# Storing kept operands later, asking for folded pieces earlier, and moving three loads in the merge of a hybrid attention and Fourier encoder layer

## The chip, the core and the metric

The kernel runs as one program on one core of a Trainium2 chip. The metric is the device time of one execution in microseconds (us); the time of the kernel before is the median of three runs. A profile of one further execution gives what every engine did and when. The engines are named as the profile names them: PE (matrix products; PEld is its weight load), DVE, ACT and POOL (element-wise work), and SP, which does nothing here but issue transfers. POOL issues some transfers too.

## The reference

Two groups of requests, a prompt of 1024 tokens and a sample of 512, go through the same layer with the same weights; 16 learned meta tokens stand in front of each. The part of the layer that matters here, cut down:

```python
h = rmsnorm(x, g_mix)
z = h @ w_in                      # 1024 -> 3*512 (q, k, v) + 512 (u) + 1024 + 1024
q, k, v, u, gate_na, gate_fn = split(z)
y_na = neighbourhood_attention(q, k, v, ...) @ w_branch_na   # 512 -> 1024
y_fn = fourier_mix(u) @ w_branch_fn                          # 512 -> 1024
mixed = sigmoid(gate_na) * y_na + sigmoid(gate_fn) * y_fn
x = x + mixed @ w_out
a = relu(rmsnorm(x, g_mlp) @ w_up)
x = x + (a * a) @ w_down          # then a last rmsnorm
# fourier_mix: real part of the 2-D DFT over (positions, the 128 channels of a group)
```

All of it is float32.

## The kernel before

**Numbers.** A float32 operand is split into a high part (rounded to the type that PE multiplies at full rate) and a low part (the rest). `split_sb` does it for data in SBUF: ACT casts the high part (L156), POOL or DVE subtracts for the low part (L158). `split_ps` does it from PSUM (L137, L138). `mm3` (L133) makes one product out of three matmuls for each contraction tile: high by high, low by high, high by low.

**Order.** The sample goes through attention, gates, Fourier part and merge first, then the prompt; the change touches the prompt alone ("not small" in the code), and there the stretch from 790 to 1050 us of the span, between the prompt's attention and its output projection. Each engine takes its instructions in an order that is fixed when the program is built: a scheduler lays them out by the dependences, by `behind(marks)` (nothing before the marked instruction of an engine) and by `pinned()` (here and nowhere else). A tile pool with `bufs=n` hands out its n buffers in turn, and a tile waits until the buffer's former user is done with it. The transfers of SP are issued in that engine's order: an instruction that waits holds all that stand behind it.

**The stretch in five steps.**

1. `gates`: the pre-activations of both gates, one block of 128 columns after another. Six of the sixteen were made earlier and are read back (L916); ten remain. A block is one weight load (`weights`, L150, `w_raw<-in_w_in`, two buffers), its split (`w_hi<-w_raw` on ACT, `w_lo` on POOL), two chunks of 512 positions with 24 matmuls each (`ps<-hT`), and two sigmoids (L934, `gate<-ps`). Between the first blocks `bring` loads the four attention outputs (`w_raw<-o_prompt`, through the same two buffers) and splits them into `oT0` to `oT3`.
   Beside the blocks runs the list `beside`: after block number `done`, one step of each generator whose range holds that number. `fold_positions` has eight such steps (0 to 7): DVE adds and subtracts the mirrored halves of the normalised input and stores the two halves in DRAM (`folded_prompt<-half`, L1071). `keep_fn` has eight (1 to 8): it loads one block of the Fourier branch's weights (`raw<-wfn`, L1025), splits it, and stores the pair (`fn<-w_hi`, `fn<-w_lo`, L1017). `bring` stores each `oT` once it is split (`oT<-oT_hi`, also L1017).
2. `merge_na`: the first `FIRST` = 2 column blocks of the attention branch's product, two of 512 positions each, 12 matmuls a product (`na_product`; weights `na0`, `na1`, loaded as `w_raw<-in_w_na` and split by ACT and POOL; the pair of buffers for `na` is shared with the pairs of `keep_fn`). After each block, four more steps of `fold_positions`: these ask for the sixteen stored pieces (`half<-folded_prompt`, L1078, three buffers) and split them into the space of `hT`, which the gates have then done with.
3. `fourier_channels`: the channel product in two parts of five groups of 128 rows. The last group of part 0 has nine rows, and they are rows of the second half. The weights `wu` come by POOL's queue (L1009).
4. `half_positions`: the position DFT, ten products; the last four use two sine tables (`sin<-in_sin_prompt`, L1207, POOL's queue), the high one from the start of each and the low one in its last five matmuls.
5. `merge_half`: eight column blocks. Each has four Fourier products (two chunks by two parts, 26 matmuls in all, weights `wf` fetched back from the `fn` tiles), and behind a block stand some of the 12 attention products that step 2 left, as a list of running totals says: `upto = (1, 3, 4, 6, 7, 9, 10, 12)`. For them `oT0` to `oT3` are fetched back (L1041): the first two by SP after part 1, into space on the left, the others once the sine tables' space is free.

Then come `project_out` and the MLP.

Of the kernel before, what the change touches and what calls it, by code (L numbers as in the profile page):

```python
# [27 lines left out]
NM = 16  # L28
# [40 lines left out]
class Layer:  # L69
# [362 lines left out]
    def run(self, order):  # L432
# [6 lines left out]
        for i, (name, T) in enumerate(order):  # L439
# [32 lines left out]
            if small:  # L472
                ap, hp_, mp = (right.enter_context(pool(f"{n}_{name}", "right")) for n in ("acc", "hid", "mlp"))
                fn = right_fn.enter_context(pool(f"fn_{name}", "right"))

                halves = [t[:, i * (NM + T) // 2:(i + 1) * (NM + T) // 2] for t in
                          [ap.tile([128, D], F32, name=f"acc{t}") for t in range(T // 128)] +
                          [hp_.tile([128, D], F32, name="hn", bufs=2) for _ in range(2)] for i in range(3)]
                temp = lambda: mp.tile([128, D], F32, name="gain", bufs=1)[:, :(NM + T) // 2]
                na = (lambda: mp.tile([128, 512], F32, name="relu", bufs=2).rearrange("p (a b) -> p a b", a=4),  # L480
                      lambda: tuple(t.rearrange("p (a b) -> p a b", a=4) for t in self.pair(hp_, [128, T], "hid", 4)))
            else:
                fn = None
                p = right_fn.enter_context(pool(f"na_{name}", "right"))
                halves = None
                temp = lambda: p.tile([128, 576], F32, name="half", bufs=3)[:, :(NM + T) // 2]
                na = (None, lambda: self.pair(p, [128, 4, 128]))
                outs = []
                keeping = self.keep_fn(p)
            hm = None  # L490
            if not small:
                hm = p.tile([128, 8, NM], F32, name="hm")
                nc.sync.dma_start(hm, self.hmeta.rearrange("k p c -> p k c"))
            fold = self.fold_positions(name, T, hT, folded, temp, halves, hm)
            beside = [(fold, 0, 8)] if small else [(fold, 0, 8), (keeping, 1, 9)]
            if small:
                wide = lambda: [fn.tile([128, n], F32R, name=f"wu{n}")[:, :1040].rearrange("p (a b) -> p a b", a=4) for n in (1040, 1072)]
                flat = lambda pair: [t.rearrange("p a b -> p (a b)") for t in pair]
# [3 lines left out]
                beside = [(*beside, 0, 1), (*beside, 2, 10), (fold, 5, 13)]  # L502

            def bring(pr):
                if pr and not small:
                    outs.append(self.keep(f"oT{pr - 1}", oT[pr - 1]))
                self.weights(od[pr], oT[pr], raw=hp_.tile([128, T], F32R, name="hid_hi", bufs=4) if small else "raw")
                if pr == 3 and not small:
                    outs.append(self.keep(f"oT{pr}", oT[pr]))

            near_end = self.gates(T, hT, mixed, sig, bring, beside)
            sin = []
# [16 lines left out]
            with pool(f"u_{name}", "right") as up:  # L529
                u, cos = self.fourier_channels(up, name, T, folded, wu, ahead, (  # L530
                    lambda: mp.tile([128, 512], F32, name="relu", bufs=2).bitcast(F32R)[:, :half_rows(NM + T) + 1]) if small else None)
                close_hT()
                fp, close_fT = self.open(f"fT_{name}", "left")
                br, close_br = (fn, lambda: None) if small else self.open(f"br_{name}", "left")
                oT = oT if small else [None] * 4

                def back(prs, place):
                    for pr in prs:
                        oT[pr] = self.fetch_kept(outs[pr], self.pair(place, [128, T], f"oT{pr}", 1))

                if not small:
                    oa, close_oa = self.open(f"oTa_{name}", "left")
                    back((0, 1), oa)
                    fn_products = self.half_products(fp, br)
                with pool(f"dft_{name}", "right") as p:
                    fT, marks = (self.fourier_positions if small else self.half_positions)(p, fp, name, T, u, cos, sin if small else sin + [
                        self.sines(p.tile([128, 5 * 522], F32R, name="sin"), name, T, 1)])
            with self.pinned():
                for _ in ahead:
                    pass  # L550
# [393 lines left out]
    def merge_na(self, places, T, hT, oT, mixed, wu, fold, ahead):  # L944
        nc = self.nc
        raw_, pair_ = places
        for dm in range(8 if raw_ else self.FIRST):
            if raw_:
                raw = raw_()
                nc.sync.dma_start(raw, self.rows("w_na", dm * 128))  # L950
                wb = self.split_sb(raw, *pair_())
            else:
                wb = self.weights(self.rows("w_na", dm * 128), pair_(), raw=self.wtile("raw", [128, 4, 128]))
            for c in range(T // 512):
                self.na_product(wb, oT, mixed, dm, c)
            for _ in range(1 if raw_ else 8 // self.FIRST):
                next(fold)
            if dm == 7:
                with self.pinned():
                    next(ahead, None)  # L960
            for n in (dm - 2,) if raw_ else (2 * dm, 2 * dm + 1):
                if not 0 <= n < 3:
                    continue
                part, k = divmod(n, 2)
                wu[part, k] = self.folded(part, k, [self.wtile("raw" if part else kind, [128, 4, 260]) for kind in ("hi", "lo")])

    FIRST = 2

    def na_product(self, wb, oT, mixed, dm, c):

# [46 lines left out]
            self.nc.sync.dma_start(d, t.bitcast(F32))  # L1017
        return kept

    def keep_fn(self, p):  # L1020

        def load(dm):
            if dm < 8:
                raws.append(p.tile([128, 4, 128], F32, name="raw", bufs=2))
                self.nc.sync.dma_start(raws[-1], self.wfn[dm])  # L1025

        raws, pairs = [], []
        load(0)
        for dm in range(8):
            load(dm + 1)  # L1030
            pairs.append(self.split_sb(raws[dm], *self.pair(p, [128, 4, 128]), lo_engine=self.nc.vector))
            if dm:
                self.kept_fn.append(self.keep(f"fn{dm - 1}", pairs[-2]))
            if dm == 7:
                self.kept_fn.append(self.keep("fn7", pairs[-1]))
            yield

    def fetch_kept(self, kept, pair):

        for d, t in zip(kept, pair):  # L1040
            self.nc.sync.dma_start(t.bitcast(F32), d)  # L1041
        return pair

    def fold_positions(self, name, T, hT, to, temp, keep, hm):

        hT, = hT
        nc = self.nc
        N = NM + T  # L1050
        M = N // 2
        to, = to
        hi, lo = hT
        kept = []
        if keep is None:
            dram = self.dram.tile([8, 2, 128, M], F32, name=f"folded_{name}")
        for kt in range(8):
            a = temp()
            b, c = (temp(), temp()) if keep is None else keep[2 * kt:2 * kt + 2]
            m = 0 if hm is None else NM  # L1060
            if m:
                nc.vector.tensor_copy(a[:, 0:m], hm[:, kt])
            for x, s in ((a[:, m:], slice(0, M - m)), (b, slice(M - m, N - m))):
                nc.vector.tensor_tensor(out=x, in0=hi[:, kt, s].bitcast(F32), in1=lo[:, kt, s].bitcast(F32), op=ALU.add)
            nc.vector.tensor_copy(c[:, 0:1], a[:, 0:1])
            nc.vector.tensor_tensor(out=c[:, 1:], in0=a[:, 1:], in1=b[:, 1:][:, ::-1], op=ALU.add)
            nc.vector.tensor_tensor(out=b[:, 1:], in0=a[:, 1:][:, ::-1], in1=b[:, 1:], op=ALU.subtract)
            kept.append((c, b))
            if keep is None:
                for i in range(2):  # L1070
                    nc.sync.dma_start(dram[kt, i], kept[kt][i])  # L1071
            yield
        for n in range(16):
            i, kt = divmod(n, 8) if keep is None else (n % 2, n // 2)
            x = kept[kt][i]
            if keep is None:
                x = temp()
                nc.sync.dma_start(x, dram[kt, i])  # L1078
            self.split_sb(x, *(t[:, kt, i * M:(i + 1) * M] for t in to), lo_engine=nc.vector)
            if n % 2:  # L1080
                yield

# [219 lines left out]
    def merge_half(self, br, T, fT, fn, oT, mixed, sig, gate, wout, marks):  # L1302
# [10 lines left out]
        def fetch(dm):  # L1313
            if dm < 8:
                w[dm] = self.fetch_kept(self.kept_fn[dm], self.pair(br, [128, 4, 128], "wf"))
            n = dm + self.FIRST
            if n < 8:
                na[n] = self.weights(self.rows("w_na", n * 128), [self.wtile(kind, [128, 4, 128]) for kind in ("hi", "lo")],
                                     raw=br.tile([128, 4, 128], F32R, name="raw", bufs=2))

        turn, self.turn = self.turn, self.turn + ["t"]
        fetch(0)
        due = 0
        for dm in range(8):
            total.append(br.tile([128, D], F32, name="hn", bufs=2)[:, :T])
# [15 lines left out]
                a, b = max(1, k0), min(M - 1, k0 + kn - 1) + 1  # L1341
                nc.vector.tensor_tensor(out=y[:, T - b + 1:T - a + 1][:, ::-1], in0=even[:, a - k0:b - k0], in1=odd[:, a - k0:b - k0], op=ALU.subtract)
            nc.vector.tensor_tensor(out=y, in0=y, in1=sg, op=ALU.mult)
            upto = (1, 3, 4, 6, 7, 9, 10, 12)[dm]
            while due < upto:
                n, c = pieces[due]
                with self.behind(self.mark(lane)):
                    self.na_product(na[n], oT, mixed, n, c)
                due += 1
            nc.vector.tensor_tensor(out=y, in0=mx, in1=y, op=ALU.add)  # L1350
            if dm % 2:
# [816 lines left out]
```

## Time and profile before

| what | value |
|---|---|
| time, median of 3 runs | 1907.04 us (1906.94 to 1907.17) |
| profiled execution | 1912.94 us, of which the span is 1911.2 us |
| granted PE clock over the span | 0.993 of full speed |
| PE busy | 1869.4 us, 98% of the span |
| DVE, ACT, POOL busy | 1111.0, 806.1, 792.4 us |
| 780 to 1050 us: PE busy | 255.70 of 270 us, clock 0.97 |
| 1049 to 1900 us: PE busy | 849.68 of 851 us, clock 1.00 |

Times within the program are microseconds from the start of the span. In a row of the timeline the columns are the start, the length, the engine, the line, the operation with its output and inputs, shapes, and the number of instructions in the row; a bracket gives the idle time of the engine just before the row and what ended it. A matmul's length overlaps the next one's, so PE's pace is read from start to start. In the view of waits the three numbers are the total in us, how often, and the longest.

### The profile page before, as it was taken

To read this page: it belongs to the slowest core of one execution; us is meant where nothing else is said; L and a number is where in the kernel's file an instruction comes from. 1 tells how busy PE (TensorE), PEld (TensorE's weight loads), DVE (VectorE), ACT (ScalarE), POOL (GpSimd) and SP (SyncE) were. 2 spreads that over 40 slices of the span, in tenths; PEclk is the share of its full clock that TensorE was granted. 3 is DMA by queue.
4 is the path that set the end of the run, shared out by engine and by line. 5 is a ranking of instruction groups with operands and counts; after the bars stand their busy time and mean duration, and the time that the engine had idled before them with its cause. 6 is when DMAs were issued, how large, how long until landed. Compare 5 with 4: busy or idle time off the path is not lost.

```text
span 1911.2 us, 25803 instructions
## 1 busy us (share of the span) xinstructions
PE 1869.4 (98%) x9155; PEld 1566.6 (82%) x9155; DVE 1111.0 (58%) x1753; ACT 806.1 (42%) x1487; POOL 792.4 (41%) x664
## 2 busy tenths in 40 slices
PE   8999999999999999999889999999999999999998
PEld 6878888888888888778888878888888888888886
DVE  5771654887625566632357376565666336657756
ACT  4884333444216778722223244333333333333434
POOL 1325643555512233333212219887872323323531
PEclk9999999999999999999999999999999999999999
DMA  7857964788755555586763423545446778668633
GB/s 228 211 132 232 250 207 140 227 267 254 232 197 162 140 147 149 187 289 174 206 214 105 155 100 133 173 157 186 151 170 246 276 252 301 219 210 307 226 115 127
DMA packets 320536, 375.19 MB, mean 196 GB/s; under 512 B 52564, under 2 KB 224468, under 8 KB 319856
## 3 DMA queue, kind: packets, MB, share of 16 engines
q1 hardware_dynamic: 301992, 351.76, 56.1%
q0 software_dynamic: 18416, 21.80, 5.1%
q8 instruction: 72, 1.18, 0.2%
q14 instruction: 56, 0.46, 0.1%
HBM read 271.50 MB, written 104.55 MB: 197 GB/s over the span
## 4 chain that ended last, share of the span: by engine, by line
PE 82%; DMA 7%; DVE 4%; ACT 4%; issue 1%; SPq 1%; POOL 1%; DVEq 0%; ACTq 0%; POOLq 0%
PE ps_o L133 21%; PE ps_mm L133 20%; PE ps_s L133 16%; PE ps_t L133 12%; PE ps_mm L645 2%; PE ps_mm L644 2%; PE ps_mm L646 2%; PE ps_o L801 1%; DMA half<-folded_prompt 1%; PE ps_t L776 1%; DMA sin<-in_sin_prompt 1%; PE ps_t L195 1%; DMA gain<-in_w_fnB 1%; ACT sc L770 0%; PE ps_s L764 0%
## 5 line engine op out<-in xcount | busy, mean ns | idle before, releaser
L158 POOL TENSOR_TENSOR w_lo<-w_raw,w_hi 128x1024 fp32r<-128x1024 f32 (+1 forms) x70 | 177.0, 2530 | 205.6 <-ACT w_hi L156 150.2
L156 ACT CAST w_hi<-w_raw 128x1024 fp32r<-128x1024 f32 (+1 forms) x90 | 93.6, 1040 | 181.8 <-PE ps_s L133 51.6
L158 POOL TENSOR_TENSOR w_lo<-raw,w_hi 128x1024 fp32r<-128x1024 f32 (+1 forms) x39 | 84.4, 2169 | 201.8 <-ACT w_hi L156 163.0
L158 DVE TENSOR_TENSOR h_lo<-long,h_hi 128x1024 fp32r<-128x1024 f32 x54 | 76.3, 1415 | 101.9 <-ACT h_hi L156 101.9
L644 PE MATMUL ps_mm<-hT,w_hi 128*128 128x512 f32 (+2 forms) x296 | 118.3, 400 | 0.2 <-DVE k L692 0.2
L156 ACT CAST h_hi<-long 128x1024 fp32r<-128x1024 f32 x54 | 56.8, 1051 | 135.6 <-PE ps_o L133 28.0
L646 PE MATMUL ps_mm<-hT,w_lo 128*128 128x512 f32 (+2 forms) x296 | 110.9, 375 | 0.0
L645 PE MATMUL ps_mm<-hT,w_hi 128*128 128x512 f32 (+2 forms) x296 | 110.8, 374 | 0.0
L158 DVE TENSOR_TENSOR hs_lo<-short,hs_hi 128x512 fp32r<-128x512 f32 x54 | 66.1, 1225 | 17.0 <-ACT hs_hi L156 15.9
L1705 POOL TENSOR_TENSOR x<-w_hi,x 128x512 fp32r<-128x512 f32 (+1 forms) x39 | 64.8, 1661 | 18.4 <-ACT x L1702 18.4
L730 POOL TENSOR_TENSOR vb<-vr,vb 96x384 fp32r<-96x384 f32 (+4 forms) x48 | 48.5, 1019 | 50.2 <-ACT vb L729 48.0
L133 PE MATMUL ps_t<-gate,x 128*128 128x512 f32 x276 | 66.5, 390 | 0.0
L646 PEld LDWEIGHTS ps_mm<-hT,w_lo 128*128 128x128 f32 x296 | 56.0, 189 | 10.2
L770 ACT ACTIVATE sc<-sc,ast 128x288 f32<-128x288 f32 (+4 forms) x96 | 53.7, 560 | 24.7 <-DVE ast L768 24.1
L156 ACT CAST w_hi<-raw 128x1024 fp32r<-128x1024 f32 (+1 forms) x47 | 39.8, 847 | 56.9 <-PE ps_mm L133 13.5
L138 DVE TENSOR_TENSOR pt<-ps_t,pt 96x384 fp32r<-96x384 f32 (+4 forms) x96 | 53.1, 554 | 18.1 <-ACT pt L137 16.8
L133 PE MATMUL ps_mm<-gate,x 128*128 128x512 f32 x256 | 63.2, 389 | 0.0
L133 PEld LDWEIGHTS ps_t<-gate,x 128*128 128x128 f32 x276 | 51.7, 188 | 10.8 <-ACT w_hi L137 0.2
L768 DVE CUSTOM_DVE_ANT_0 sc<-ps_s,bm 128x288 f32<-128x288 f32 (+4 forms) x96 | 46.3, 482 | 22.4 <-PE ps_s L764 14.6
L156 ACT CAST hs_hi<-short 128x512 fp32r<-128x512 f32 x54 | 33.5, 621 | 59.5 <-PE ps_mm L133 19.9
L645 PEld LDWEIGHTS ps_mm<-hT,w_hi 128*128 128x128 f32 x296 | 56.6, 191 | 1.7
L644 PEld LDWEIGHTS ps_mm<-hT,w_hi 128*128 128x128 f32 x296 | 56.4, 190 | 2.0 <-PE ps_s L764 0.3
(789 smaller groups left out, 5581.5 us busy)
## 6 DMA issues: line engine op xcount, KB each, us to landing
long<-hidden_prompt SPq DMA_DIRECT2D x54, 512.0 KB
w_raw<-in_w_in SPq DMA_DIRECT2D x52, 512.0 KB
raw<-in_w_down SPq DMA_DIRECT2D x39, 512.0 KB
w_raw<-in_w_up SPq DMA_DIRECT2D x34, 512.0 KB
hidden_prompt<-h SPq DMA_DIRECT2D x32, 512.0 KB
short<-hidden_sample SPq DMA_DIRECT2D x54, 256.0 KB
w_lo<-in_w_down SPq DMA_DIRECT2D x18, 512.0 KB
w_raw<-in_w_out SPq DMA_DIRECT2D x16, 512.0 KB
```

Source lines behind the costliest of these rows:

```text
L133: self.nc.tensor.matmul(out, a, b, start=(i == 0 and not more), stop=(i == len(terms) - 1), skip_group_check=more)
L138: self.nc.vector.tensor_tensor(out=lo, in0=ps, in1=(hi if ref is None else ref).bitcast(F32), op=ALU.subtract)
L156: nc.scalar.copy(out=hi, in_=raw)
L158: (lo_engine or nc.gpsimd).tensor_tensor(out=lo, in0=raw, in1=hi.bitcast(F32), op=ALU.subtract)
L195: nc.tensor.transpose(tp[:, i * 128:i * 128 + n], hn[:n, kt * 128:(kt + 1) * 128], self.ident[:n, :n])
L644: nc.tensor.matmul(ps, a[0], b[0], start=(kt == 0), stop=False)
L645: nc.tensor.matmul(ps, a[0], b[1], start=False, stop=False)
L646: nc.tensor.matmul(ps, a[1], b[0], start=False, stop=(kt == 7))
L730: nc.gpsimd.tensor_tensor(out=lo, in0=vs, in1=hi.bitcast(F32), op=ALU.subtract)
L768: nc.vector.tensor_tensor_reduce(out=sc[:, :W], in0=ps[:, :W], in1=bm[:, :W], scale=1.0, scalar=3e38, op0=ALU.add, op1=ALU.min, accum_out= ...
L770: nc.scalar.activation(out=sc[:, :W], in_=sc[:, :W], func=AF.Exp, bias=st[:, 0:1], scale=-1.0, accum_out=st[:, 1:2])
L1705: (engine or self.nc.gpsimd).tensor_tensor(out=w[1], in0=raw, in1=w[0].bitcast(F32), op=ALU.subtract)
```

## The change

It has five parts.

- `keep_fn` becomes `keep_beside`: one raw buffer instead of two, its steps stand after blocks 3 to 9 instead of 1 to 8, each step loads the next weights after its stores, and the `oT` pairs are stored by the last four steps instead of by `bring`.
- `fold_positions` asks for pieces ahead: four buffers of 528 columns instead of three of 576; a ninth step after block 8 issues the first four loads, and each split is followed by the load four pieces on.
- `FIRST` = 3: three attention column blocks (six products) stand in front of the Fourier part and five (ten products) are left for `merge_half`, with `upto = (0, 1, 2, 4, 6, 7, 9, 10)`. Three steps of the fold stand after each of the three; the first two pairs of `wu` are asked for after the first block, the third after the last.
- `oT0` and `oT1` come back by POOL's queue, behind the second sine table, instead of by SP.
- In `merge_half` the attention weights are asked for two column blocks ahead of use, apart from `wf`.

```diff
-                temp = lambda: p.tile([128, 576], F32, name="half", bufs=3)[:, :(NM + T) // 2]
+                temp = lambda: p.tile([128, 528], F32, name="half", bufs=4)[:, :(NM + T) // 2]
-                keeping = self.keep_fn(p)
+                keeping = self.keep_beside(p, lambda: p.tile([128, 4, 128], F32, name="raw", bufs=1), oT, outs)
-            beside = [(fold, 0, 8)] if small else [(fold, 0, 8), (keeping, 1, 9)]
+            beside = [(fold, 0, 8)] if small else [(fold, 0, 9), (keeping, 3, 10)]
             def bring(pr):
-                if pr and not small:
-                    outs.append(self.keep(f"oT{pr - 1}", oT[pr - 1]))
                 self.weights(od[pr], oT[pr], raw=...)
-                if pr == 3 and not small:
-                    outs.append(self.keep(f"oT{pr}", oT[pr]))
...
-                    back((0, 1), oa)
...
+                    if not small:
+                        sin.append(self.sines(p.tile([128, 5 * 522], F32R, name="sin"), name, T, 1))
+                        with self.behind(self.mark((mybir.EngineType.Pool,))):
+                            back((0, 1), oa, nc.gpsimd)
...
-            for _ in range(1 if raw_ else 8 // self.FIRST):
-                next(fold)
+            for _ in range(1 if raw_ else 3):
+                next(fold, None)
-            for n in (dm - 2,) if raw_ else (2 * dm, 2 * dm + 1):
+            for n in (dm - 2,) if raw_ else (0, 1) if dm == 0 else (2,) if dm == self.FIRST - 1 else ():
-    FIRST = 2
+    FIRST = 3
...
+    def keep_beside(self, p, raw, oT, outs):
         for dm in range(8):
-            load(dm + 1)
             pairs.append(self.split_sb(raws[dm], *self.pair(p, [128, 4, 128]), lo_engine=self.nc.vector))
             if dm:
                 self.kept_fn.append(self.keep(f"fn{dm - 1}", pairs[-2]))
+            load(dm + 1)
             if dm == 7:
                 self.kept_fn.append(self.keep("fn7", pairs[-1]))
-            yield
+            if dm > 3:
+                outs.append(self.keep(f"oT{dm - 4}", oT[dm - 4]))
+            if dm:
+                yield
...
+        for n in range(4):
+            load(n)                       # half<-folded_prompt, piece n
+        if keep is None:
+            yield
         for n in range(16):
-            if keep is None:
-                x = temp()
-                nc.sync.dma_start(x, dram[kt, i])
+            x = kept[kt][i] if keep else xs[n]
             self.split_sb(x, *(t[:, kt, i * M:(i + 1) * M] for t in to), lo_engine=nc.vector)
+            load(n + 4)
...
+        for n in range(2):
+            fetch_na(self.FIRST + n)
-            upto = (1, 3, 4, 6, 7, 9, 10, 12)[dm]
+            upto = (0, 1, 2, 4, 6, 7, 9, 10)[dm]
                     self.na_product(na[n], oT, mixed, n, c)
+                if c:
+                    fetch_na(n + 2)
```

How the order of instructions changes is shown at three places. In the rows a name like `fn_8609` is one DRAM tile or buffer; `x2` stands for two instructions of a kind in a row.

First, SP, where the third and the fourth of the attention outputs are asked for between the gates' blocks. Before:

```order
L1071 DMA folded_prompt<-half 128x520 x2
L1025 DMA raw<-wfn_2838 128x512
L1017 DMA fn_8609<-w_hi 128x512
L1017 DMA fn_8610<-w_lo 128x512
L1017 DMA oT_8620<-oT_hi 128x1024
L1017 DMA oT_8621<-oT_lo 128x1024
L150 DMA w_raw<-o_prompt_5492 128x1024
L1071 DMA folded_prompt<-half 128x520 x2
L1025 DMA raw<-wfn_2849 128x512
L1017 DMA fn_8697<-w_hi 128x512
L1017 DMA fn_8698<-w_lo 128x512
L150 DMA w_raw<-in_w_in 128x8x128
```

After the change the same place reads:

```order
L150 DMA w_raw<-o_prompt_5491 128x1024
L150 DMA w_raw<-in_w_in 128x8x128
L1075 DMA folded_prompt<-half 128x520 x2
L150 DMA w_raw<-o_prompt_5492 128x1024
L1075 DMA folded_prompt<-half 128x520 x2
L150 DMA w_raw<-in_w_in 128x8x128
L1075 DMA folded_prompt<-half 128x520 x2
L1023 DMA raw<-wfn_2787 128x512
L150 DMA w_raw<-o_prompt_5493 128x1024
L150 DMA w_raw<-in_w_in 128x8x128 x3
```

The gate weight behind `o_prompt_5492`, the fifth of the ten, now has two stores of the fold between itself and that load; the stores of `fn` and `oT` stand further down.

Second, ACT at the end of the gates. Before, the first two attention weights are cast ahead of the pieces:

```order
L156 CAST w_hi_9089<-raw_9021 128x512
L156 CAST w_hi_9159<-w_raw_9161 128x512
L156 CAST w_hi_9233<-w_raw_9235 128x512
L934 ACTIVATE gate_8359<-ps_mm_9107 128x512
L156 CAST hT0_3758<-half_9193 128x520
L156 CAST hT0_3758<-half_9197 128x520
L156 CAST hT0_3758<-half_9201 128x520
L934 ACTIVATE gate_8359<-ps_s_9133 128x512
```

After (`w_hi_9151` is the last of the Fourier weights, `w_hi_9167`, `w_hi_9233` and `w_hi_9291` are the three attention weights):

```order
L932 ACTIVATE gate_8359<-ps_mm_9099 128x512
L156 CAST hT0_3758<-half_9071 128x520
L156 CAST hT0_3758<-half_9073 128x520
L156 CAST hT0_3758<-half_9075 128x520
L932 ACTIVATE gate_8359<-ps_s_9125 128x512
L156 CAST w_hi_9151<-raw_9087 128x512
L156 CAST w_hi_9167<-w_raw_9169 128x512
L156 CAST hT0_3758<-half_9077 128x520
L156 CAST hT0_3758<-half_9203 128x520
L156 CAST hT0_3758<-half_9207 128x520
L156 CAST w_hi_9233<-w_raw_9235 128x512
```

The cast of the first attention weight now stands behind three casts of pieces, the last sigmoid of the gates and the last Fourier weight; the second stands behind three more pieces.

Third, POOL at the end of the DFT. Before, nothing but splits follows the second sine table:

```order
L1207 DMA sin<-in_sin_prompt 128x5x256
L1207 DMA sin<-in_sin_prompt 128x5x266
L158 TENSOR_TENSOR w_lo<-raw,w_hi 128x512 x3
L158 TENSOR_TENSOR hid_lo<-w_raw,hid_hi 128x1024
L158 TENSOR_TENSOR w_lo<-raw,w_hi 128x512 x2
```

After:

```order
L1221 DMA sin<-in_sin_prompt 128x5x256
L1221 DMA sin<-in_sin_prompt 128x5x266
L1045 DMA oT_hi<-oT_8926 128x1024
L1045 DMA oT_lo<-oT_8927 128x1024
L1045 DMA oT_hi<-oT_9009 128x1024
L1045 DMA oT_lo<-oT_9010 128x1024
L158 TENSOR_TENSOR w_lo<-raw,w_hi 128x512 x2
```

The four loads of `oT0` and `oT1` have moved from SP, where they stood ahead of the first `wf`, to POOL's queue behind the table; `oT2` and `oT3` stay on SP. On PE, `merge_half` now begins with the Fourier products of two column blocks and then has one attention product, where it had one block and one attention product.

More of the change, by code (lines that the diff above doesn't have):

```diff
@@ L535, in run, with back @@
                 oT = oT if small else [None] * 4
-                def back(prs, place):
+                def back(prs, place, queue=None):
                     for pr in prs:
-                        oT[pr] = self.fetch_kept(outs[pr], self.pair(place, [128, T], f"oT{pr}", 1))
+                        oT[pr] = self.fetch_kept(outs[pr], self.pair(place, [128, T], f"oT{pr}", 1), queue)
                 if not small:
                     oa, close_oa = self.open(f"oTa_{name}", "left")
-                    back((0, 1), oa)
                     fn_products = self.half_products(fp, br)
                 with pool(f"dft_{name}", "right") as p:
-                    fT, marks = (self.fourier_positions if small else self.half_positions)(p, fp, name, T, u, cos, sin if small else sin + [
-                        self.sines(p.tile([128, 5 * 522], F32R, name="sin"), name, T, 1)])
+                    if not small:
+                        sin.append(self.sines(p.tile([128, 5 * 522], F32R, name="sin"), name, T, 1))
+                        with self.behind(self.mark((mybir.EngineType.Pool,))):
+                            back((0, 1), oa, nc.gpsimd)
+                    fT, marks = (self.fourier_positions if small else self.half_positions)(p, fp, name, T, u, cos, sin)
             with self.pinned():
@@ L1018, in keep @@
         return kept
-    def keep_fn(self, p):
+    def keep_beside(self, p, raw, oT, outs):
         def load(dm):
             if dm < 8:
-                raws.append(p.tile([128, 4, 128], F32, name="raw", bufs=2))
+                raws.append(raw())
                 self.nc.sync.dma_start(raws[-1], self.wfn[dm])
@@ L1033, in keep_fn, with fetch_kept @@
                 self.kept_fn.append(self.keep(f"fn{dm - 1}", pairs[-2]))
+            load(dm + 1)
             if dm == 7:
                 self.kept_fn.append(self.keep("fn7", pairs[-1]))
-            yield
-    def fetch_kept(self, kept, pair):
+            if dm > 3:
+                outs.append(self.keep(f"oT{dm - 4}", oT[dm - 4]))
+            if dm:
+                yield
+    def fetch_kept(self, kept, pair, queue=None):
         for d, t in zip(kept, pair):
-            self.nc.sync.dma_start(t.bitcast(F32), d)
+            if queue is None:
+                self.nc.sync.dma_start(t.bitcast(F32), d)
+            else:
+                queue.dma_start(t, d)
         return pair
@@ L1072, in fold_positions, with load @@
             yield
+        xs = []
+        def load(n):
+            if keep is None and n < 16:
+                i, kt = divmod(n, 8)
+                xs.append(temp())
+                nc.sync.dma_start(xs[-1], dram[kt, i])
+        for n in range(4):
+            load(n)
+        if keep is None:
+            yield
         for n in range(16):
             i, kt = divmod(n, 8) if keep is None else (n % 2, n // 2)
-            x = kept[kt][i]
-            if keep is None:
-                x = temp()
-                nc.sync.dma_start(x, dram[kt, i])
+            x = kept[kt][i] if keep else xs[n]
             self.split_sb(x, *(t[:, kt, i * M:(i + 1) * M] for t in to), lo_engine=nc.vector)
+            load(n + 4)
             if n % 2:
@@ L1315, in fetch, with fetch_na @@
                 w[dm] = self.fetch_kept(self.kept_fn[dm], self.pair(br, [128, 4, 128], "wf"))
-            n = dm + self.FIRST
+        def fetch_na(n):
             if n < 8:
```

## The prediction

> **What bounds the kernel now.** I read the busy time by stretches first, then PE's waits, then the timeline at each wait.
>
> ```profile
> 780.00:1050.00 270.00, 255.70 (x1383) 219.46 (x1382) 126.92 (x199) 88.14 (x147) 70.13 (x55) 0.97 0.64 199
> 1049.00:1900.00 851.00, 849.68 (x3797) 702.58 (x3796) 505.94 (x568) 304.55 (x463) 414.89 (x222) 1.00 0.56 195
> ```
>
> The columns are the stretch, its length, busy time of PE, PEld, DVE, ACT and POOL, PE's granted clock, the DMA engines' share and GB/s. From 1049 on PE is idle for 1.3 us in 851: whatever ends the merge earlier ends the program earlier by as much. The stretch that the change touches has 14.3 us of idle PE and a clock of 0.97. PE's waits there, those of two windows and the largest of a third (1000 to 1140), say where:
>
> ```profile
> PE ps_o L133 <- ACT w_hi L156: 3.0, 1, 3.0
> ...
> PE ps_s L133 <- ACT hT L156: 4.9, 4, 2.2
> PE ps_o L133 <- DMA oT_hi<-oT: 2.3, 2, 1.6
> PE ps_o L133 <- DMA oT_lo<-oT: 1.6, 2, 1.0
> PE ps_o L133 <- DMA sin<-in_sin_prompt: 1.3, 1, 1.3
> ...
> PE ps_s L1561 <- DVE gate L138: 0.8, 1, 0.8
> ```
>
> Four places, 13.1 us. Each costs more than its idle time, since PE's pace is slow behind some. So I price them from start to start, against undisturbed work of the same kind.
>
> **What is removed.** (a) The fifth gate weight.
>
> ```profile
> 829.88 3.79 PE L133 MATMUL ps_s<-hT,w_hi 128*128 128x512 f32 x16
> 845.43 3.79 PE L133 MATMUL ps_mm<-hT,w_hi 128*128 128x512 f32 x16
> 850.87 0.39 PE L133 MATMUL ps_s<-hT,w_hi 128*128 128x512 f32 x1
> 831.21 0.44 SPq L150 DMA_DIRECT2D w_raw<-in_w_in  x1
> 837.43 1.04 ACT L156 CAST w_hi<-w_raw 128x1024 fp32r<-128x1024 f32 x1 [0.81 <-DMA w_raw<-in_w_in]
> ```
>
> A chunk takes 850.87 − 845.43 = 5.44 us; the two from 829.88 to 845.43 took 15.55, so 4.67 too many. The load was issued at 831.21, behind stores of `fn` and `oT`, and cast 6.2 us later. With those stores later, the load stands behind two stores of the fold alone. Between nothing and 2.5 us may stay, if the fold's subtraction on DVE, for which those stores wait, is itself late; I take 0.3, since DVE loses a split of `fn` in each of the blocks before.
>
> (b) The fold's last pieces, which the fifth group of part 0 needs.
>
> ```profile
> 925.09 0.28 PE L133 MATMUL ps_mm<-w_hi,hT 128*128 128x260 f32 x1
> 927.98 0.28 PE L133 MATMUL ps_s<-w_hi,hT 128*9 128x260 f32 x1
> 941.55 1.10 PE L133 MATMUL ps_mm<-w_raw,hT 128*128 128x252 f32 x8
> 944.34 1.10 PE L133 MATMUL ps_s<-w_raw,hT 128*128 128x252 f32 x8
> 905.27 26.79 SPq L1078 DMA_DIRECT2D half<-folded_prompt  x13
> ```
>
> A group of part 0 takes 2.89, one of part 1 2.79; the two from 927.98 to 941.55 took 13.57, 7.9 too many. Thirteen of the sixteen piece loads were issued from 905.27 to 932.06, about 2.1 us apart, each when one of three buffers came free. Now four stand in SBUF when the gates end, and two more products (2 × 2.72 us, below) lie ahead of the group that needs them: it falls about 25 us behind the gates' end instead of 22.7. At 2.1 us a piece the twelve others are done in 25, and with four buffers sooner; I take the whole 7.9 as gained.
>
> (c) The second sine table.
>
> ```profile
> 963.55 2.20 PE L133 MATMUL ps_s<-sin,us 128*128 128x256 f32 x15
> 969.03 1.94 PE L133 MATMUL ps_mm<-sin,us 128*128 128x256 f32 x15
> 972.65 0.28 PE L1295 MATMUL ps_o<-fx,wx 96*128 96x256 f32 x1
> 953.14 1.72 POOL L1207 DMA_DIRECT2D sin<-in_sin_prompt  x2 [1.12 <-PE ps_mm L133]
> 953.12 0.35 SPq L1041 DMA_DIRECT2D oT_hi<-oT  x1
> ```
>
> Two products took 5.48 where the next two took 3.62: 1.86 too many. Its issue is bound to the end of part 1, as before. What changes is who shares the transfer time: four loads of `oT` went out on SP beside it, the first at 953.12, and now two pairs come behind it on its own queue. It was issued at 953.14 and the wait ended at 968.3, 15 us later; without those 2 MB (at the 199 GB/s of the stretch 10 us of all engines) about 11 are enough. It may keep 0 to 1.86; I take 0.5.
>
> (d) `oT2` and `oT3` at the first attention product of the merge.
>
> ```profile
> 975.80 0.39 PE L133 MATMUL ps_o<-oT_hi,w_hi 128*128 128x512 f32 x1
> 989.43 0.39 PE L133 MATMUL ps_mm<-oT_hi,w_hi 128*128 128x512 f32 x1
> 992.15 0.39 PE L133 MATMUL ps_s<-oT_hi,w_hi 128*128 128x512 f32 x1
> 972.85 0.34 SPq L1041 DMA_DIRECT2D oT_hi<-oT  x1
> 982.45 0.80 PE L133 MATMUL ps_o<-oT_lo,w_hi 128*128 128x512 f32 x1 [0.58 <-DMA oT_lo<-oT]
> ```
>
> An attention product is 2.72 (992.15 − 989.43), a Fourier block 3.15 (975.80 − 972.65); one of each took 13.63, 7.76 too many. The loads were issued at the DFT's end, 972.85, and the last was used 9.6 us later. Now a second Fourier block stands in front: the last `oT` pair is wanted 2 × 3.15 + 1.6 = 7.9 us after the DFT, so about 1 us may stay; at worst 4, if the first `wf` and the POOL queue's two pairs share the time. I take 1.0.
>
> Sum removed: 4.67 + 7.9 + 1.86 + 7.76 = 22.2 us. The products themselves are as many as before.
>
> **What is added.** The first attention product waits for a cast that now stands last in a row on ACT.
>
> ```profile
> 905.27 0.39 PE L133 MATMUL ps_o<-oT_hi,w_hi 128*128 128x512 f32 x1
> 903.88 1.68 ACT L156 CAST hT<-half 128x520 fp32r<-128x520 f32 x3 [1.66 <-PE ps_s L133]
> 905.47 0.60 ACT L934 ACTIVATE gate<-ps_s 128x512 f32<-128x512 f32 x1
> 895.72 0.32 SPq L1017 DMA_DIRECT2D fn<-w_hi  x1
> 901.10 0.62 ACT L156 CAST w_hi<-w_raw 128x512 fp32r<-128x512 f32 x1 [4.89 <-issue]
> ```
>
> The last sigmoid starts 0.2 us after PE's last gate matmul (905.47 against 905.27). Behind it come the last `fn` cast and then `na0`'s, each about 0.5 us after the one before: `na0` is ready 0.2 + 0.5 + 0.5 + 0.6, some 1.9 us after PE wants it. This is in the order, so I count it whole: 1.9 us of idle PE that was not there.
>
> Idle PE can bring a slower clock, and the rows disagree on when:
>
> ```profile
> 97.58 0.88 PE L776 MATMUL ps_t<-ident,sc 128*96 128x128 f32 x3 [2.31 <-ACT sc L772]
> 97.50:100.50 3.00, 2.92 (x14) 2.91 (x15) 2.36 (x10) 2.72 (x10) 0.42 (x2) 0.50 0.87 244
> 931.04 0.29 PE L133 MATMUL ps_s<-w_hi,hT 128*9 128x260 f32 x1 [1.94 <-ACT hT L156]
> 931.00:934.00 3.00, 1.21 (x6) 0.30 (x6) 2.01 (x3) 1.21 (x2) 0.40 (x1) 0.93 0.42 106
> ```
>
> After 2.31 us idle the clock was 0.50 for three us, which costs 1.5; after 1.94 it stayed at 0.93. The wait of 1.9 is nearest to the second; I take 0.6, range 0 to 1.5. The Trainium skill, "TensorE: Matmul & The Clock Gate", section on the HAM clock gate, has the half clock only after an idle window of about 3.4 us: by that rule the 0.6 would be nothing, and the time 0.6 lower. The row at 97.58 speaks against it here.
>
> `na1` shares its two buffers with the `fn` pairs, so its cast waits until the last `fn` pair has landed. Before, that store was issued at 895.72 and the cast followed at 901.10, 5.4 us. Now the store follows the cast of the last pair, about 1.5 us after the gates' end, so `na1` is ready near 6.9 after it and is wanted at 1.9 + 2 × 2.72 = 7.3. It fits by 0.4; the range is 0 to 2, I take 0.5. `na2` has the pair of `na0` and five us more: 0.2 (0 to 1.5).
>
> The merge is now nearly as long for DVE as for PE:
>
> ```profile
> 985.00:1049.00 64.00, 64.00 (x361) 56.82 (x361) 50.30 (x63) 20.29 (x31) 15.89 (x8) 0.97 0.31 99
> 1038.75 0.69 DVE L975 TENSOR_TENSOR gate<-ps_t,gate 128x512 f32<-128x512 f32 x1 [2.03 <-PE ps_t L133]
> 1040.81 2.36 DVE L1355 TENSOR_TENSOR gate<-hn,gate 128x1024 fp32r<-128x1024 f32 x2
> ```
>
> DVE had 50.3 us of work in 64 and at the end waited 2.0 us for PE, then took 4.4 us (1038.75 to 1043.17), while PE worked on with earlier blocks and waited 0.8. Two attention products less are 1.4 us less DVE work, but the merge loses 7.8 us of stall and 5.4 of products: some 55 us of DVE work then stand in about 56. I take 0.7 for it, range 0 to 3.
>
> The stores of `fn` and `oT` that moved cost nothing by themselves: they lie beside the last six blocks (each 2 × 5.44 us of PE), in a stretch whose DMA share is 0.64. If that cover is gone, the next gate weight is late as in (a), up to 4.67.
>
> Sum added and left: 0.3 + 0.5 + 1.0 + 1.9 + 0.6 + 0.5 + 0.2 + 0.7 = 5.7. Net 22.2 − 5.7 = 16.5. The profiled execution was 1912.94, so 1896.4 for a profiled one; the median stands 5.9 lower (1907.04), hence **1890.5 us**. With each addition at its low end but the certain 1.9, it is 1886.7.
>
> **The rivals.** *The front of the attention product costs more.* `na1` waits on a store's landing, `na2`'s load stands behind piece loads on SP, and each wait of over 2 us brings the half clock as at 97.58. For it: three weights share two pairs and ACT's one row. Against it: the products give each 5.4 us. Price: 2 + 1.5 + 1.5 + 1.5 above my 0.7 and 0.6, some 5 us: 1892.5 to 1897.
>
> *The transfers come no earlier.* All queues' bytes cross the same engines, so four loads moved from SP to POOL may slow the table or `oT2` and `oT3` as before. For it: in (d) 2 MB needed 9.6 us. Against it: share 0.31 in the merge. (c) would keep 1.86 and (d) 5: 1892 to 1897. The Trainium skill, "DMA: Bandwidth & Descriptors", section "Issuing engines are not separate DMA queues", says that transfers of all issuing engines end on the same 16 DMA engines; by that rule the move to POOL gives no bandwidth, and only the order counts.
>
> *Slower.* The stores that were spread over nine blocks now crowd the last six on SP, each waiting for its split; `na0`'s load stands behind twelve of them. If it is issued late, PE waits with nothing to do, and the pieces behind it are late as well. It must be issued within some 6 us (the transfer in (a)) of PE's need, and each us later is one lost. It gives a slower program only from 17 us late, so later than 11 us behind the gates' end. DVE and ACT are busy for 127 and 88 of 270 us there, so I see no reason for such a backlog: 1908 to 1915.
>
> *The waits change places.* If the engine behind all four is the transfer rate, what is gained in (a) returns in (b) and so on: within 4 us of 1907. A share of 0.64 speaks against it.
>
> **How the numbers follow.** Forecast 0.62 (own range 1886.7 to 1893); front 0.17; transfers 0.14; changed places 0.04; slower 0.03. Low is 1886.5, just below the sum with low ends. High reaches to the ends of the second and third, and a little beyond for both together, 1898. A measurement of this kernel can tell some 0.2%, 3.8 us: faster 0.94 (the first three and a little off), same 0.03, slower 0.03.
>
> **What would show it.** In the profile after: no wait of PE on the cast of a gate weight; the nine-row group as long as its neighbours; one PE wait of about 1.9 us on the cast of `w_hi` at the gates' end; no wait over 1 us on `sin` or `oT` loads; merge end near 1022 instead of 1038.6; DVE without idle time in the merge. Wrong would be: a new PE wait above 2 us in the gates' last six blocks, or a half clock in the front products, or PE waiting on DVE after the merge by over 3 us.

## The result and the profile after

The changed kernel takes 1894.57 us (median of four runs, 1892.39 to 1895.69) against 1907.11 (1906.94 to 1910.55): ratio 0.9929, 95% interval 0.9911 to 0.9946. That is 12.5 us less, where 16.5 was forecast. 1894.57 lies inside the whole range (1886.5 to 1898), but 1.6 above the forecast's own (1886.7 to 1893), in the stretch that the prediction gave to two rivals. The two profiled executions lie further apart than the medians: 1912.94 before, 1894.29 after, 18.65 us.

PE's waits in the profile after, from 780 to 900 and from 900 to 1000, and the largest from 1000 to 1140:

```profile
PE ps_o L799 <- DVE pt L138: 0.6, 2, 0.4
PE ps_mm L133 <- DVE w_lo L158: 0.4, 1, 0.4
...
PE ps_o L133 <- ACT w_hi L156: 1.7, 1, 1.7
PE ps_s L133 <- DMA oT_lo<-oT: 0.7, 1, 0.7
PE ps_s L133 <- ACT w_hi L156: 0.6, 1, 0.6
...
PE ps_s L1580 <- DVE gate L138: 0.8, 1, 0.8
```

The waits on the gate weight's cast, on the pieces and on the sine table are gone. Of that on `oT`, 0.7 us is left. New are the two on the casts of the first and the second attention weight. The stretch and the merge as a whole (both in the columns explained in the prediction), then PE's start of each place and the end of the chain on ACT, in the timeline after:

```profile
900.00:1000.00 100.00, 97.15 (x673) 88.79 (x674) 56.14 (x91) 31.55 (x60) 32.09 (x39) 1.00 0.78 234
965.60:1019.40 53.80, 53.06 (x330) 47.65 (x329) 46.06 (x64) 17.16 (x30) 10.60 (x5) 1.00 0.47 162
828.97 3.79 PE L133 MATMUL ps_s<-hT,w_hi 128*128 128x512 f32 x16
834.41 3.79 PE L133 MATMUL ps_o<-hT,w_hi 128*128 128x512 f32 x16
839.85 3.79 PE L133 MATMUL ps_mm<-hT,w_hi 128*128 128x512 f32 x16
897.87 1.98 PE L133 MATMUL ps_s<-hT,w_lo 128*128 128x512 f32 x8
901.56 0.50 PE L133 MATMUL ps_o<-oT_hi,w_hi 128*128 128x512 f32 x1 [1.71 <-ACT w_hi L156]
904.41 0.39 PE L133 MATMUL ps_mm<-oT_hi,w_hi 128*128 128x512 f32 x1
907.85 0.50 PE L133 MATMUL ps_s<-oT_hi,w_hi 128*128 128x512 f32 x1 [0.55 <-ACT w_hi L156]
910.91 0.40 PE L133 MATMUL ps_o<-oT_hi,w_hi 128*128 128x512 f32 x1
930.66 0.28 PE L133 MATMUL ps_mm<-w_hi,hT 128*9 128x260 f32 x1
933.50 1.09 PE L133 MATMUL ps_s<-w_raw,hT 128*128 128x252 f32 x8
958.30 1.97 PE L133 MATMUL ps_mm<-sin,us 128*128 128x256 f32 x15
961.95 1.94 PE L133 MATMUL ps_o<-sin,us 128*128 128x256 f32 x15
971.87 0.39 PE L133 MATMUL ps_s<-oT_hi,w_hi 128*128 128x512 f32 x1
978.97 0.39 PE L133 MATMUL ps_o<-oT_hi,w_hi 128*128 128x512 f32 x1
900.89 0.62 ACT L156 CAST w_hi<-w_raw 128x512 fp32r<-128x512 f32 x1
```

From start to start: the chunk behind the fifth weight takes 5.44 us, the nine-row group 2.84, two sine products 3.65 (958.30 to 961.95): nothing is left at (a), (b) and (c). At (d), 978.97 − 971.87 = 7.10 where 5.87 is undisturbed: 1.2 left. At the front, the gates' last matmuls start at 0.23 us each from 897.87, so the first product was due at 899.7 and came 1.9 later; the second column block was due at 907.13 and came 0.7 later; the first and third products run 0.5 longer together. In sum 4.3 us. The granted clock is 1.00 there. The merge ends at 1019.4, where near 1022 was expected. DVE works for 46.06 of its 53.8 us and waits several times for PE (0.7 to 1.8 us each).

### The profile page after: what moved, and what is told of

It reads as the page before. It is cut to its first block, busy times and chain, and to the rows that moved or that the text cites. A ratio compares the mean times of both kernels' runs of the same rounds, so it can differ in the third digit from the quotient of the medians.

```text
span 1892.2 us, 25804 instructions
## 1 busy us (share of the span) xinstructions
PE 1859.7 (98%) x9155; PEld 1559.5 (82%) x9155; DVE 1106.5 (58%) x1753; ACT 805.7 (43%) x1487; POOL 792.5 (42%) x668
## 4 chain that ended last, share of the span: by engine, by line
PE 85%; DVE 4%; ACT 4%; DMA 4%; issue 1%; POOL 1%; SPq 0%; DVEq 0%; ACTq 0%; POOLq 0%
PE ps_o L133 22%; PE ps_mm L133 21%; PE ps_s L133 17%; PE ps_t L133 12%; PE ps_mm L643 2%; PE ps_mm L642 2%; PE ps_mm L644 2%; PE ps_o L799 1%; PE ps_t L774 1%; ACT sc L768 1%; PE ps_t L195 1%; ACT w_hi L156 1%; ACT sc L770 1%; PE ps_s L762 1%; PE ps_s L761 0%
## 5 line engine op out<-in xcount | busy, mean ns | idle before, releaser
L158 DVE TENSOR_TENSOR hs_lo<-short,hs_hi 128x512 fp32r<-128x512 f32 x54 | 65.8, 1219 | 17.6 <-ACT hs_hi L156 16.5
L138 DVE TENSOR_TENSOR pt<-ps_t,pt 96x384 fp32r<-96x384 f32 (+4 forms) x96 | 53.1, 554 | 17.8 <-ACT pt L137 16.5
```

The lines of the kernel that those rows point to most:

```text
L138: self.nc.vector.tensor_tensor(out=lo, in0=ps, in1=(hi if ref is None else ref).bitcast(F32), op=ALU.subtract)
L158: (lo_engine or nc.gpsimd).tensor_tensor(out=lo, in0=raw, in1=hi.bitcast(F32), op=ALU.subtract)
```

## The experiments

The theory to test was that each part takes away its own wait and that nothing else gains or loses. The fifth part, attention weights asked for two blocks ahead, was not undone by itself, so what it is worth is not shown. Two questions stood against it: why the medians moved 6 us less than the profiles, and whether each part is needed.

**The kernel before, again.** No edit.

> The kernel before, unchanged, profiled once more. Two theories on why the medians lie 12.5 us apart while the two profiled executions lie 18.6 apart. Theory V (the four waits vary from run to run): the profiled execution shown was one with long waits; a new profile whose execution takes 1907 has the same four waits priced at 16 to 17 us instead of 22.2, with fewer half-clock stretches. Theory P (the profile adds a constant 5.9 to the kernel before): the new profiled execution is again near 1913 with some 22 us at the four places, and what is missing in the timed runs is lost to something that the profile of the changed kernel does not show. Ratio to before 1.000 by both.

Measured: 1907.15 us (1904.74 to 1911.22 in 12 runs), ratio 0.999 (0.9978 to 1.0001); the profiled execution took 1908.17, span 1906.4. PE's rows at the four places in this second profile of before:

```profile
829.88 3.79 PE L133 MATMUL ps_s<-hT,w_hi 128*128 128x512 f32 x16
846.37 3.79 PE L133 MATMUL ps_mm<-hT,w_hi 128*128 128x512 f32 x16
928.64 0.28 PE L133 MATMUL ps_s<-w_hi,hT 128*9 128x260 f32 x1
931.01 0.29 PE L133 MATMUL ps_s<-w_hi,hT 128*9 128x260 f32 x1 [1.02 <-ACT hT L156]
931.85 0.29 PE L133 MATMUL ps_s<-w_hi,hT 128*9 128x260 f32 x1 [0.43 <-ACT hT L156]
932.87 0.29 PE L133 MATMUL ps_s<-w_hi,hT 128*9 128x260 f32 x1 [0.61 <-ACT hT L156]
936.87 1.10 PE L133 MATMUL ps_mm<-w_raw,hT 128*128 128x252 f32 x8
933.00:937.00 4.00, 4.00 (x36) 3.76 (x35) 4.00 (x14) 1.29 (x5) 2.18 (x9) 1.00 0.53 136
958.87 2.26 PE L133 MATMUL ps_s<-sin,us 128*128 128x256 f32 x15
964.42 1.94 PE L133 MATMUL ps_mm<-sin,us 128*128 128x256 f32 x15
971.18 0.39 PE L133 MATMUL ps_o<-oT_hi,w_hi 128*128 128x512 f32 x1
984.57 0.39 PE L133 MATMUL ps_mm<-oT_hi,w_hi 128*128 128x512 f32 x1
```

Priced as in the prediction: (a) 16.49 − 10.88 = 5.6, (b) 8.23 − 5.68 = 2.5, (c) 5.55 − 3.6 = 1.9, (d) 13.39 − 5.87 = 7.5; 17.6 where the first profile had 22.2. The two executions differ by 4.8 us and the four places by 4.6. (b) alone is 5.4 shorter, and (a) is 0.9 longer. The pieces came earlier: the wait was 2.1 (three pieces in turn) instead of 4.9, and the clock stayed at 1.00 behind it. In the first profile the waits went on to 935.20, and the clock fell:

```profile
934.00:937.00 3.00, 1.80 (x9) 1.14 (x10) 1.82 (x7) 1.73 (x5) 1.03 (x3) 0.50 0.68 179
937.00:941.00 4.00, 4.00 (x23) 3.91 (x22) 2.68 (x9) 0.36 (x1) 2.23 (x11) 0.57 0.01 2
```

Theory V holds, as far as two profiles can show it.

**Stores early again.** The changed kernel with the kept pairs after blocks 1 to 7, and `oT` stored in `bring`:

```diff
-            beside = [...] else [(fold, 0, 9), (keeping, 3, 10)]
+            beside = [...] else [(fold, 0, 9), (keeping, 1, 8)]
```

> The changed kernel with the kept pairs stored early again (seven steps after blocks 1 to 7, the attention outputs stored as they are brought). Forecast: the fifth gate weight again stands behind stores of fn and oT, so a PE wait of about 3 us and a slow clock return there, +3.5 to +4.7; but the casts of the first two attention weights then stand ahead of the pieces on ACT, so the waits of 1.7 and 0.55 at the front of the attention product go, -2.3. Net +1 to +2.5 against the changed kernel, 1895.5 to 1897 us. Rival: the late stores are what makes the gates' end short of transfer time, and without them the pieces come earlier too: net 0 or below, 1892 to 1894.5.

Measured: 1897.85 us, ratio 0.9942 (0.9925 to 0.996), 3.3 to 3.6 above the changed kernel's two medians, more than expected. Its wait at the fifth weight, in the timeline:

```profile
830.99 3.79 PE L133 MATMUL ps_s<-hT,w_hi 128*128 128x512 f32 x16
840.90 6.36 PE L133 MATMUL ps_o<-hT,w_hi 128*128 128x512 f32 x16 [4.31 <-ACT w_hi L156]
848.91 1.29 PE L133 MATMUL ps_mm<-hT,w_hi 128*128 128x512 f32 x5
```

17.92 − 10.88 = 7.0 us are lost, more than either profile of before lost, and no wait on a cast is left at the front (3.1 gained): +3.9. This profile is of the slowest of six executions (1900.31), 6.0 above the changed kernel's profiled one; the other 2.0 lie ahead of the first place (830.99 against 828.97). So 3.9 accounts for this execution, and is not to be set against the difference of the medians. The sign of the theory holds; I had sized the wait by before's. The stores of `fn` and of `oT` moved together, so which of them delays the load stays open.

**Pieces on demand.** Three buffers, and each piece asked for one ahead:

```diff
-        for n in range(4):
+        for n in range(1):
             load(n)
-            load(n + 4)
+            load(n + 1)
```

> The changed kernel with three buffers of 576 for the pieces and each load asked for only one piece ahead of its split. Theory that the early requests are what removes the fold's wait: the nine-row group waits again for pieces, 2 to 5 us with half clock (less than the 7.9 of before since two more products stand ahead), 1896 to 1900. Rival, that the two additional products ahead of the Fourier part suffice: no wait there, within 1 us of the changed kernel.

Measured: 1894.72 us, ratio 0.9925 (0.9909 to 0.9942), the same waits as the changed kernel's. The theory fell: with late stores and `FIRST` = 3 in place, the early requests are not needed to remove (b).

**`oT0` and `oT1` on SP.** `back((0, 1), oa)` ahead of `half_products`, as before:

> The changed kernel with oT0 and oT1 fetched by SP ahead of the first wf, beside the second sine table, as before. Theory that the sharing of transfer time makes the table late: a PE wait on sin of 1 to 2 us returns, 1895.5 to 1897. Rival, that the table is on time since nothing else is late any more: no change over 0.5 us. All engines' loads end up in the same transfer engines, so the later oT2 and oT3 should be no later than in the changed kernel (0.7 us of wait).

Measured: 1896.48 us, ratio 0.9934 (0.9916 to 0.9952), some 2 us above the changed kernel's two medians. Its waits have one row that the changed kernel's have not, the first; below them, the starts of the first and the third sine product:

```profile
PE ps_s L133 <- DMA sin<-in_sin_prompt: 1.2, 1, 1.2
PE ps_s L133 <- DMA oT_lo<-oT: 0.7, 1, 0.7
957.46 2.34 PE L133 MATMUL ps_mm<-sin,us 128*128 128x256 f32 x15
962.96 1.94 PE L133 MATMUL ps_o<-sin,us 128*128 128x256 f32 x15
```

The two products take 5.50, 1.9 too many, as in before. So the table is late when four loads of `oT` go out beside it, and on time when they go out behind it; the wait on the later `oT` is the same in both. What moved is the queue of the four loads, and with it their order and their time of issue.

**The changed kernel, again.** No edit.

> The changed kernel, unchanged, as the reference for its neighbours and to see how much its executions scatter. If the scatter of the kernel before (1904 to 1914) comes from the fold's wait with or without a half clock, the changed kernel, which has no such wait, scatters over 3 to 4 us only, with a median of 1894 to 1895; if the scatter comes from outside the four places, it is as wide as before's.

Measured: 1894.24 us (1892.0 to 1894.7 in 5 runs), ratio 0.9924 (0.9911 to 0.9936); before, timed beside it, 1908.37 (1905.08 to 1911.22). The gain is thus 14.1 us here and 12.5 in the first comparison. The scatter is 2.7, a little less than the 3 to 4 expected.

**Two blocks in front.** `FIRST = 2`, five fold steps after each block, `upto = (0, 2, 4, 6, 7, 9, 10, 12)`:

> The changed kernel with FIRST = 2 as before, so four attention products in front and twelve in the merge (running totals 0, 2, 4, 6, 7, 9, 10, 12, so still two Fourier blocks ahead of the first); the early requests for pieces stay. Theory F (the two more products in front are what hides the fold): the nine-row group waits again, 1 to 3 us, 1896 to 1899. Theory E (the early requests do it, and each of the two would do alone, as the run with pieces on demand leaves open): no wait there, within 1 us of the changed kernel, since the products are only moved.

Measured: 1893.26 us, ratio 0.9921 (0.9909 to 0.9933); no wait at the nine-row group. With the early requests in place, `FIRST = 3` is not needed either.

**Neither.** Both edits together:

> The changed kernel with neither of the two that each alone left the nine-row group without a wait: FIRST = 2 with two Fourier blocks in front in the merge, and three buffers of 576 with each piece asked for one ahead. If either of the two is needed to hide the fold, its wait returns: 2 to 5 us, with or without a half clock, 1896 to 1900 and a wider scatter. Rival: with the late stores out of the way and the first pieces asked for in the gates' last block, the fold is on time without both, and the time stays within 1 us of 1893.3.

Measured: 1893.73 us, ratio 0.9921 (0.9907 to 0.9934), with 0.2 us of wait at the group. The rival is right as far as the time goes.

**Kept pairs one block earlier.**

```diff
-            beside = [...] else [(fold, 0, 9), (keeping, 3, 10)]
+            beside = [...] else [(fold, 0, 9), (keeping, 2, 9)]
```

> The changed kernel with the steps of the kept pairs after blocks 2 to 8 instead of 3 to 9. The casts of the first two attention weights then stand ahead of the pieces on ACT. Forecast: the two waits at the gates' end (1.7 and 0.55 us) go, the fifth gate weight stays in time since no store stands ahead of it, -2 to -2.5 against the changed kernel: 1892 to 1893. Rival: a store of fn then delays a gate weight (the sixth or seventh) by up to 4 us, net +2.

Measured: 1889.96 us (1889.68 to 1890.43), ratio 0.9904 (0.9889 to 0.9919): 4.3 us less than the changed kernel timed beside it, no two runs overlapping. Both waits at the front are gone and no gate weight is late. That is some 2 us more than expected: the expectation counted idle time at the front (2.3), which from start to start had cost 3.1, and (d) became shorter too:

```profile
968.27 0.39 PE L133 MATMUL ps_s<-oT_hi,w_hi 128*128 128x512 f32 x1
974.79 0.39 PE L133 MATMUL ps_o<-oT_hi,w_hi 128*128 128x512 f32 x1
```

6.52 − 5.87 = 0.65 is lost there, where the changed kernel lost 1.2.

**No cover.** That kernel with `FIRST = 2` and pieces on demand:

> The kernel of the run before last but three (kept pairs one block earlier, so no wait at the front of the attention product) with neither FIRST = 3 nor the early requests: two attention blocks in front, each piece asked for one ahead, three buffers. In the run with neither, PE's waits of 1.7 and 0.6 us at the front gave the fold time, and the last piece was cast as the nine-row group began. Theory (the new wait at the front hid what the fold still lacked): without the front's waits the nine-row group waits 1.5 to 3 us for pieces, 1891.5 to 1894. Rival (the late stores alone put the fold on time): no wait there, 1889.5 to 1890.5.

Measured: 1889.85 us (1888.93 to 1893.92), ratio 0.99 (0.9882 to 0.9919). In its profile:

```profile
899.20 0.39 PE L133 MATMUL ps_o<-oT_hi,w_hi 128*128 128x512 f32 x1
923.52 0.62 ACT L156 CAST hT<-half 128x520 fp32r<-128x520 f32 x1 [1.33 <-DMA half<-folded_prompt]
924.20 0.29 PE L133 MATMUL ps_s<-w_hi,hT 128*9 128x260 f32 x1 [0.74 <-ACT hT L156]
921.98 0.86 POOL L1221 DMA_DIRECT2D sin<-in_sin_prompt  x1 [10.41 <-PE ps_mm L133]
```

The wait is back, but 0.7 instead of 1.5 to 3, and the time is the one that the rival forecast: the front's waits hid only that much. The last piece is cast 24.3 us after the gates' end (923.52 − 899.20), where the two profiles of before needed 29.3 (934.52 − 905.27) and 26.0. One difference can be read: the first sine table is asked for at 921.98, behind the pieces, and in before at 917.62, between them. That it shortened the fold was not tried by itself, and the stores were moved as well.

**Early requests alone.** `keeping` at 2 to 9, `FIRST = 2`, four pieces ahead:

> The same with the early requests (four buffers, four pieces asked for in the gates' last block) and FIRST = 2. If the early requests alone are enough, no wait at the nine-row group and 1889.5 to 1890.5, as with FIRST = 3. If the two more products in front are needed as well, a wait of 1 us or more there, 1891 to 1892.5.

Measured: 1888.95 us (1888.14 to 1889.29), ratio 0.9891 (0.9874 to 0.9908), the best version run, 20 us below before and 0.9 below the version with no cover, both timed beside it; half a microsecond better than expected. Its stretch and its waits from 780 to 1060:

```profile
900.00:1000.00 100.00, 100.00 (x699) 92.48 (x699) 57.90 (x95) 30.91 (x59) 26.89 (x35) 1.00 0.76 232
PE ps_o L799 <- DVE pt L138: 0.7, 1, 0.7
PE ps_mm L133 <- DVE w_lo L158: 0.5, 1, 0.5
920.03 0.63 ACT L156 CAST hT<-half 128x520 fp32r<-128x520 f32 x1 [0.88 <-DMA half<-folded_prompt]
921.57 0.28 PE L133 MATMUL ps_s<-w_hi,hT 128*9 128x260 f32 x1
```

PE is busy without a gap in this stretch, and the last piece is cast before the group begins.

**One Fourier block ahead.** `upto = (1, 2, 3, 4, 6, 7, 9, 10)` in the changed kernel:

> The changed kernel with running totals 1, 2, 3, 4, 6, 7, 9, 10 in the merge: one Fourier block instead of two ahead of the first attention product. Theory that the second block is what hides oT2 and oT3: the wait on them grows from 0.7 by 3.15 to about 4 us, and a half clock adds 1 to 1.5: +3.5 to +5, 1898 to 1899.5. Rival, that they come earlier anyway since oT0 and oT1 left SP: +1 or less.

Measured: 1899.15 us, ratio 0.9951 (0.9938 to 0.9963), 4.9 more than the changed kernel timed beside it. In the timeline, with the clock behind the waits:

```profile
969.88 0.51 PE L133 MATMUL ps_s<-oT_hi,w_hi 128*128 128x512 f32 x1 [0.63 <-DMA oT_hi<-oT]
971.10 0.50 PE L133 MATMUL ps_s<-oT_lo,w_hi 128*128 128x512 f32 x1 [0.72 <-DMA oT_lo<-oT]
972.34 0.50 PE L133 MATMUL ps_s<-oT_hi,w_hi 128*128 128x512 f32 x1 [0.74 <-DMA oT_hi<-oT]
973.57 0.56 PE L133 MATMUL ps_s<-oT_lo,w_hi 128*128 128x512 f32 x1 [0.73 <-DMA oT_lo<-oT]
975.00:979.50 4.50, 4.50 (x28) 4.31 (x28) 1.14 (x3) 0.75 (x2) 0.00 (x0) 0.75 0.00 0
```

Each of the four loads is waited for in turn, 2.8 us in all where 4 was expected, and the clock is 0.75 after. So the second block is what hides `oT2` and `oT3`.

**Before with three blocks in front.** `FIRST = 3`, `upto = (1, 2, 3, 4, 6, 7, 9, 10)`, three fold steps after each block, all else as before:

> The kernel before with only the fold's place changed: three attention blocks in front (six products), running totals 1, 2, 3, 4, 6, 7, 9, 10 in the merge, three fold steps after each; early stores, pieces, sine table and oT as before. If the two more products hide the fold, its wait (2.5 us in the second profile of before, 7.9 in the first) goes, the other three stay: 1902 to 1905, and, if the scatter of before comes from that wait, executions within 4 us instead of 10. Rival: the fold is no more than two products late in the good executions only; then 0.5 to 2 us of wait stay in some and the scatter too.

Measured: 1904.37 us (1902.26 to 1908.19 in 11 runs), ratio 0.9982 (0.9974 to 0.9991): the group's wait is gone, the other three stay. The scatter is 5.9, that of before beside it 5.4. The expectation on it is refuted: the scatter does not come from the fold alone.

## Why the prediction was right, and where it was off

The mechanism held at each place, but for the reason given at (b), on which more below. (a), (b) and (c) went whole, where 0.3, nothing and 0.5 were left to remain. (d) kept 1.2 for 1.0. The first weight's wait cost 1.9, as worked out from ACT's row; the second's 0.7 for 0.5; the third's nothing for 0.2. The slower clock (0.6) did not come, and 0.5 of longer products stands in its place. DVE cost nothing for 0.7: PE's wait on it after the merge is 0.8 in both profiles, and DVE was not without idle time, as it had some 50 us of work up to its last instruction of the merge, where the prediction had 55. Sum 4.3 for 5.7. The Trainium skill ("TensorE: Matmul & The Clock Gate", section on the HAM clock gate) has the half clock after an idle window of about 3.4 us. This wait of 1.71 us agrees with that; the clock of 0.75 behind the short waits of one Fourier block ahead does not, and neither does the prediction's own row at 97.58. By the profiles the net is 22.2 − 4.3 = 17.9, measured 19.0 between the spans, of which 0.9 lies ahead of the first place (829.88 against 828.97).

The step that failed is the last: "the median stands 5.9 lower (1907.04), hence 1890.5". It took the distance between the profiled execution and the median for a constant, beside the waits. The second profile of before shows that most of it is itself wait: two executions 4.8 us apart differ by 4.6 at the four places. So the waits have to come off the execution that they were seen in: 1912.9 − 22.2 + 4.3 = 1895.0 by the first profile, 1908.2 − 17.6 + 4.3 = 1894.9 by the second, against a median of 1894.57. The size of the term removed was read from an execution that was slower than the median by that very term. That the time still lay inside the whole range is owed to the rivals' share of it, which stood for a dearer front and late transfers; as neither came, it is luck.

Two readings in the working were off without harm. The reading "after 1.94 it stayed at 0.93" stops before the last wait at that place (2.18 us, up to 935.20): from 934 to 937 the clock was 0.50, and this slow stretch is a good part of the 7.9 of (b). And the nine-row group does not fall about 25 us behind the gates' end: 22.7 and two products of 2.72 make 28.1, which left the pieces more room than was claimed.

One point was right for the wrong reason: (b) was credited to early requests and two more products. Each alone leaves no wait (early requests with late stores, the two products also with early ones), and late stores with neither leave 0.2 to 0.7 us. The parts overlap, so the gain of 2.5 to 7.9 us can't be shared out among them.

None of the rivals accounts for the miss, though the time lies where two of them put it (1892 to 1897): the front cost 3.1 us, 0.1 less than in the sum; the table and the later `oT` were on time or nearly so, no wait changed place, and no gate weight was late. The front's 3.1 and the 1.2 of (d), 4.3 in sum, are what the version with early requests alone no longer has; it lies 5.3 below the changed kernel, which was timed at another time.

## What to carry to other kernels

Before a sum of waits is set against a median, see whether the profiled execution is itself one with long waits: price the waits from two or three profiles, and take them off the execution they were seen in. Where several parts of a change hide the same wait, undo them one at a time and then together, since each can be idle. And when stores are put off to let a load through, look at what they land in front of: here one block earlier was worth 4.3 us more.

## What the runs showed of the hardware

Scatter went with waits on transfers: executions of before spread over 1903.3 to 1914.2 us in all comparisons, those of the changed kernel over 1892.0 to 1895.7, and the five of the version without such a wait over 1.2. That the waits cause the whole scatter is not shown: the version with no cover, with one wait of 0.7, spread over 5.0 in six. And the clock falls not only after one long wait. Four waits of 0.63 to 0.74 us within 4.3 us left it at 0.75, while one of 1.71 (after) left it at 1.00, and three of 1.02, 0.43 and 0.61 within 2.9 us (the second profile of before) did so too.
